# Weight loads issued by GpSimd instead of SyncE, and a later place for readers of fresh transfers, in a two-layer decoder step

## Chip, core and metric

The kernel runs on one core of a Trainium2 chip. The metric is the device time of one execution in microseconds (us), given as the median of three runs. In the views, PE is TensorE (its matmuls), PEld its weight loads, DVE VectorE, ACT ScalarE, POOL GpSimd, and SP SyncE, which here does nothing but issue DMAs. "SPq" and "POOLq" are the queues of instructions of these engines. L190 is the line of the program at which the scheduler of the kernel before calls every instruction, so nearly all rows have this line, and the tile names tell them apart.

## What is computed

One inference step of a two-layer hybrid decoder for a prompt of 512 tokens and, with the same weights, 8 further sequences of one token each (together T = 520 columns). The width is 1024.

```python
def hgrn2_chunked(q, g, k, v, S0):
    # S_t = diag(f_t) S_{t-1} + k_t v_t^T, o_t = S_t^T q_t, with g = log f, k = 1 - f
...
def hgrn2_mixer(xn, w_in, lb, onorm_g, w_out, S0):
    q, fpre, i, z = jnp.split(xn @ w_in, 4, axis=-1)
    q = jax.nn.silu(q)
    f = lb + (1.0 - lb) * jax.nn.sigmoid(fpre)
    o, S = hgrn2_chunked(heads(q), heads(jnp.log(f)), heads(1.0 - f), heads(i), S0)
    o = rmsnorm(o, onorm_g) * jax.nn.silu(z)
    return o @ w_out, S
...
def trunk(x, p, pos, hgrn_state, k_past, v_past, ...):
    for l in range(DEPTH):                      # DEPTH = 2
        xn = rmsnorm(h, pre_norm_g[l])
        if l < N_A_LAYERS:                      # layer 0: HGRN2, 16 heads of 128
            mix, S = hgrn2_mixer(xn, w_in_a[l], lb_all[l], onorm_a[l], w_out_a[l], S0)
        else:                                   # layer 1: 32 query heads of 64, 4 K/V heads, window 128
            k_sh, v_sh = jnp.split(rmsnorm(h, kv_norm_g) @ w_kv, 2, axis=-1)
            q, z = jnp.split(xn @ w_in_b[j], 2, axis=-1)
            o = window_attn_prompt(rope(q), rope(k_sh), v_sh, sinks[j])    # or window_attn_sample
            mix = (o * jax.nn.silu(z)) @ w_out_b[j]
        h = h + rmsnorm(mix, post_norm_g[l])
        h = h + (p[l] @ w_pe[l]) * jax.nn.sigmoid(h @ w_pg[l])
```

All inputs and outputs are float32.

## The kernel before

**Tiles.** Activations lie with their features on the 128 partitions and the 520 tokens along a row; a 1024-wide activation is eight such tiles. A projection makes one 128-row block of its output at a time: for each of the eight chunks of the contraction it multiplies a 128x128 block of weights with the activations, in two halves of 260 columns (`Step.mm`). To keep float32 accuracy, weights and activations are each split into a high and a low part, and three products are summed: high by high, low weight by high, high weight by low. In the rows these are `pj<-xs,wh`, `pj<-xs,wl` and again `pj<-xs,wh`, each twice for the two halves.

**Weights.** One raw weight tile `wr` is 128x1024 float32, 512 KB, and holds the eight 128x128 blocks of one output block. There are three `wr` buffers. `Step.piece` (line 600) issues its load and has `Step.halves` (line 641) split it in two pieces of 512 columns: ACT casts the piece to the high part `wh`, then DVE or POOL subtracts to get the low part `wl` (`nc.either`, which lets the scheduler choose between the two). A raw buffer is free once both of its pieces are split. Four buffers hold `wh`, four `wl`; weights of `spare` kind use tiles of another pool. `Step.stream` (line 566) walks over all output blocks and enters the pieces ahead of their use as the buffers allow. The first two pieces are special: piece 0 comes in two quarters (`begin_piece`), piece 1 in a half load.

**The first layer.** For each of 16 heads four projections (q, f, v, z) are streamed, and beside them runs the chain of an earlier head (`Step.hgrn`, line 964): scaled copies and masked products, and products `ph` on TensorE. Some operands must be transposed. `Step.turn` (line 914) does it by a round trip through memory: DVE transposes blocks into `tmp`, one DMA writes `tmp` to the DRAM tile `td`, and four DMAs read it back into `xr`. The part for the 8 sequences (`sample_a`) has further transfers of up to 512 KB (`sd`, `sb`, `in_state`). The head's norm ends in a power on POOL (`hnr`). Then follow the product with W_out, the norm over all features (`rstd`, with the power `rsr` on POOL between two products of TensorE) and the gate by `w_pe` and `w_pg`. The second layer has the same frame around windowed attention. The norm is done for the two halves of the columns apart, so `rsr` occurs twice for each norm.

**What sets the order.** Nothing is issued while the program is written. `Plan.enter` records every operation with its dependences and a price for each engine that may run it; `Plan.issue` (line 231) then simulates the whole program. It has a clock for each engine, chooses at each step the operation that can begin first (`choose`, line 259; ties go by level and by age), advances the clock by its price, and issues it. What results is one fixed list of instructions per engine, and each engine works through its list in order; an instruction that waits holds up all behind it. A DMA takes 0.45 us of its queue's clock, and its data are taken to be there 1.6 us after a modelled pipe has moved them. For TensorE `choose` already puts back operations whose operands were ready for less than HAND = 0.3 us. `self.second` is the number of the operation with which the second layer begins, `low` the oldest operation not yet issued. All DMAs are issued by SP, 777 of them; 151 are loads of `wr`.

Of the kernel before, what the change touches and what calls it, by code (L numbers as in the profile page):

```python
# [55 lines left out]
LAT = {"tensor": 0.28, "vector": 0.2, "scalar": 0.25, "gpsimd": 0.17}  # L56
HAND = 0.3

BEGIN = {"tensor": 0.9, "vector": 0.8, "scalar": 2.0, "gpsimd": 0.7, "sync": 0.0}

IDLE, SLOW = 3.4, 6.8
LATE = 1.5

RUNS = ((64, 4.0), (128, 2.0), (256, 1.4), (512, 1.15))
BACKLOG, CALM = 1.5, 40.0
# [27 lines left out]
class Plan:  # L93
# [46 lines left out]
    def price(self, engine, op, aps, a, k):  # L140


        size = max(int(np.prod(x.shape[1:])) for x in aps)
        if engine == "sync":
            run = min(self.run(x) for x in aps)
            return aps[0].nbytes() / 3.3e5 * next((f for n, f in RUNS if run <= n), 1.0), False
# [33 lines left out]
        t = 0.07 + 0.00104 * size + part  # L180
# [4 lines left out]
    def enter(self, on, name, a, k):  # L185
# [4 lines left out]
        op = Op(len(self.ops), self.level, on, [lambda c=c: c(*a, **k) for c in calls],  # L190
                [self.price(e, name, ins, a, k) for e in on], on[0] == "sync")
        if any(x.tensor.name.startswith("tw") for x in ins[1:]):
# [38 lines left out]
    def issue(self):  # L231
# [27 lines left out]
        def choose(e):  # L259
# [12 lines left out]
            able = [x for x in able if x[0] <= t]  # L272
            able.sort(key=lambda x: (e == "tensor" and x[2] + HAND > t, rank[x[1].level], x[1].n))
            if e == "gpsimd":
# [20 lines left out]
        while todo:  # L295
# [16 lines left out]
            if op.dma:  # L312
                t = max(t, lanes[0])
                clock[e] = t + 0.45
                pipe = max(pipe, t + 1.4) + cost
                op.end = pipe + 1.6 + op.late
                lanes = lanes[1:] + [op.end]
            else:
                if e == "tensor":
                    if t - clock[e] > IDLE:  # L320
                        slow = t + SLOW
                    if t < slow:
                        cost *= 2
                op.end = clock[e] = t + cost
                if held:
                    port = op.end
                    stale.update(("vector", "gpsimd"))
# [119 lines left out]
class Step:  # L447
# [152 lines left out]
    def piece(self, order, n):  # L600
# [6 lines left out]
        if w.raw is None or n < 2:  # L607
# [3 lines left out]
            sl = slice(cols[0] * PIECE, (cols[-1] + 1) * PIECE)  # L611
            self.nc.sync.dma_start(w.raw[:, sl], w.src[:, sl])
        w.pieces[half] = self.halves(w.raw[:, half * PIECE : (half + 1) * PIECE], w.spare)
# [1219 lines left out]
```

## Time and profile before

| what | value |
|---|---|
| median of 3 runs | 1070.82 us |
| lowest, highest | 1068.94, 1073.45 us |
| profiled execution, its own time | 1070.85 us |
| span of its trace | 1069.1 us |
| instructions in the span | 23985 |
| moved by the DMA queues | 178.99 MB, mean 167 GB/s |

The profiled execution's time is longer than its span by what lies before the first and after the last recorded instruction. The chain that ended last, followed back from the end of the program, is split by engine, and by the instructions with the largest shares:

```profile
PE 80%; DVE 7%; ACT 4%; DMA 4%; SPq 2%; issue 2%; POOLq 0%; POOL 0%; ACTq 0%; DVEq 0%
PE pj L190 62%; PE ph L190 18%; SPq L190 2%; DVE tmp L190 1%; DMA xr<-td 1%; DVE wl L190 1%; DVE xr L190 1%; ACT g L190 1%; ACT sb L190 1%; DVE g L190 1%; ACT wh L190 1%; DMA g<-pe 1%; DVE b L190 1%; DMA sb<-in_state 1%; ACT og L190 1%
```

A row of grouped instructions reads: line, engine, operation, what it writes <- what it reads, shape, count | busy us in all, mean ns of one | us of idle time of the engine just before them, and who ended most of it. A row of the instructions in order reads: start in us, duration, engine, line, operation, and in brackets the idle time before it and who ended it. A row of a table by windows reads: window, its length, and busy us (and count) of PE, PEld, DVE, ACT and POOL, then the granted clock of TensorE, the mean busy share of the DMA engines and GB/s. A row of a wait view reads: who waited <- for whom: us in all, times, longest us.

### The profile page before, as it was taken

To read this page: it belongs to the slowest core of one execution; us is meant where nothing else is said; L and a number is where in the kernel's file an instruction comes from. 1 tells how busy PE (TensorE), PEld (TensorE's weight loads), DVE (VectorE), ACT (ScalarE), POOL (GpSimd) and SP (SyncE) were. 2 spreads that over 40 slices of the span, in tenths; PEclk is the share of its full clock that TensorE was granted. 3 is DMA by queue.
4 is the path that set the end of the run, shared out by engine and by line. 5 is a ranking of instruction groups with operands and counts; after the bars stand their busy time and mean duration, and the time that the engine had idled before them with its cause. 6 is when DMAs were issued, how large, how long until landed. Compare 5 with 4: busy or idle time off the path is not lost.

```text
span 1069.1 us, 23985 instructions
## 1 busy us (share of the span) xinstructions
PE 1057.8 (99%) x8828; PEld 1051.2 (98%) x8828; DVE 905.4 (85%) x1971; ACT 684.1 (64%) x1829; POOL 111.7 (10%) x190
## 2 busy tenths in 40 slices
PE   9999999999999999999999999999999999999998
PEld 8999999999999999999999999999999999999998
DVE  8898788874877858778889999699999998999894
ACT  7877667665767647677736565477667654675542
POOL 1111111101111002111110000000100000002000
PEclk9999999999999999999999999999999999999999
DMA  9566656664756647676664454644433556423422
GB/s 302 185 199 199 175 167 216 191 195 142 221 155 208 195 140 217 181 209 194 198 200 160 151 190 136 176 115 138 122 103 118 156 156 190 147 89 117 162 100 81
DMA packets 147069, 178.99 MB, mean 167 GB/s; under 512 B 76932, under 2 KB 99660, under 8 KB 146952
## 3 DMA queue, kind: packets, MB, share of 16 engines
q1 hardware_dynamic: 146952, 177.46, 54.7%
q8 instruction: 70, 1.15, 0.5%
q14 instruction: 47, 0.39, 0.1%
HBM read 137.04 MB, written 34.86 MB: 161 GB/s over the span
## 4 chain that ended last, share of the span: by engine, by line
PE 80%; DVE 7%; ACT 4%; DMA 4%; SPq 2%; issue 2%; POOLq 0%; POOL 0%; ACTq 0%; DVEq 0%
PE pj L190 62%; PE ph L190 18%; SPq L190 2%; DVE tmp L190 1%; DMA xr<-td 1%; DVE wl L190 1%; DVE xr L190 1%; ACT g L190 1%; ACT sb L190 1%; DVE g L190 1%; ACT wh L190 1%; DMA g<-pe 1%; DVE b L190 1%; DMA sb<-in_state 1%; ACT og L190 1%
## 5 line engine op out<-in xcount | busy, mean ns | idle before, releaser
L190 PE MATMUL pj<-xs,wh 128*128 128x260 f32 (+2 forms) x3264 | 556.8, 285 | 1.5 <-ACT xs L190 1.3
L190 PEld LDWEIGHTS pj<-xs,wh 128*128 128x128 f32 x3264 | 458.4, 189 | 2.9 <-ACT xs L190 2.0
L190 PE MATMUL pj<-xs,wl 128*128 128x260 f32 (+2 forms) x1632 | 340.7, 285 | 0.0
L190 PEld LDWEIGHTS pj<-xs,wl 128*128 128x128 f32 x1632 | 255.2, 188 | 0.2
L190 ACT CAST wh<-wr 128x512 fp32r<-128x512 f32 x287 | 176.6, 619 | 107.7 <-PE pj L190 97.4
L190 DVE TENSOR_TENSOR wl<-wr,wh 128x512 fp32r<-128x512 f32 x273 | 186.6, 685 | 55.9 <-ACT wh L190 54.8
L190 PE MATMUL pj<-og,wh 128*128 128x260 f32 x1056 | 183.3, 285 | 0.5 <-ACT og L190 0.5
L190 PEld LDWEIGHTS pj<-og,wh 128*128 128x128 f32 x1056 | 149.7, 188 | 1.3 <-ACT og L190 0.7
L190 PE MATMUL pj<-og,wl 128*128 128x260 f32 x512 | 106.3, 284 | 0.4 <-DVE wl L190 0.4
L190 PEld LDWEIGHTS pj<-og,wl 128*128 128x128 f32 x512 | 79.9, 188 | 0.6 <-DVE wl L190 0.6
L190 ACT ACTIVATE sb<-sb,g 128x128 f32<-128x128 f32 x128 | 65.8, 560 | 6.6 <-DVE sb L190 6.6
L190 ACT ACTIVATE sb<-sb,nv 128x128 f32<-128x128 f32 x128 | 62.6, 559 | 0.3
L190 ACT COPY b<-g 128x256 f32<-128x256 f32 (+1 forms) x112 | 40.6, 377 | 20.4 <-DVE g L190 16.3
L190 ACT ACTIVATE b<-b,an 128x129 f32<-128x129 f32 x128 | 50.6, 398 | 4.6 <-DVE an L190 4.4
L190 ACT ACTIVATE tmp<-pj 128x520 f32<-128x520 f32 (+2 forms) x48 | 24.4, 526 | 41.8 <-PE pj L190 41.7
L190 PE MATMUL ph<-xs,b 128*128 128x256 f32 (+1 forms) x360 | 50.9, 283 | 0.0
L190 ACT COPY b<-ph 128x256 f32<-128x256 f32 (+1 forms) x80 | 27.9, 351 | 35.8 <-PE ph L190 35.2
L190 DVE TENSOR_TENSOR xr<-xr,b 128x256 f32<-128x256 f32 x96 | 40.8, 425 | 10.6 <-PE ph L190 8.2
L190 DVE COPY_PREDICATED xr<-lmask,ph 128x256 f32<-128x256 int32 x96 | 46.9, 489 | 3.0 <-PE ph L190 2.4
L190 PE MATMUL ph<-xr,b 128*128 128x128 f32 x320 | 48.8, 275 | 0.4 <-ACT b L190 0.4
L190 DVE TENSOR_TENSOR g<-g,b 128x256 f32<-128x256 f32 x96 | 41.1, 429 | 9.0 <-ACT b L190 5.7
L190 DVE TENSOR_TENSOR x<-x,pj 128x520 f32<-128x520 f32 (+2 forms) x64 | 39.6, 624 | 9.9 <-PE pj L190 9.2
(221 smaller groups left out, 1742.5 us busy)
## 6 DMA issues: line engine op xcount, KB each, us to landing
wr<-in_w_in_a SPq DMA_DIRECT2D x64, 512.0 KB, 4.6
sb<-sd SPq DMA_DIRECT2D x32, 512.0 KB, 5.5
wr<-in_w_in_b SPq DMA_DIRECT2D x32, 512.0 KB, 3.9
td<-tmp SPq DMA_DIRECT2D x45, 256.0 KB, 2.6
xr<-td SPq DMA_DIRECT2D x180, 64.0 KB, 3.8
sb<-in_state SPq DMA_DIRECT2D x16, 512.0 KB, 4.9
out_st_s<-sb SPq DMA_DIRECT2D x16, 512.0 KB, 3.2
wr<-in_w_out_a SPq DMA_DIRECT2D x16, 512.0 KB, 5.1
```

The source lines that it names most:

```text
L190: op = Op(len(self.ops), self.level, on, [lambda c=c: c(*a, **k) for c in calls], [self.price(e, name, ins, a, k) for e in on], on[0] == " ...
```

## The change

Two things are changed. First, `piece` issues the load of a raw weight by GpSimd's DMA queue from piece 3 on; pieces 0 to 2 stay on SP. 151 DMAs go to POOL's list, and SP keeps 626. In the scheduler, prices and the mark of a DMA now go by the operation's name instead of by the engine, and a DMA advances the clock of its queue by `ISSUE` (0.45 us on SP as before, 1.1 us on GpSimd). Second, in the first layer and after 40 us of simulated time, an operation for TensorE, VectorE or ScalarE that depends on a transfer whose planned arrival is less than SAFE = 1.5 us ago stands behind the other operations that could begin at the same moment. What each instruction computes is as before.

```diff
 SAME = {"tensor": -0.3, "vector": 0.05, "scalar": 0.1, "gpsimd": 0.02}
 LAT = {"tensor": 0.28, "vector": 0.2, "scalar": 0.25, "gpsimd": 0.17}
 HAND = 0.3
+SAFE = 1.5
+SHY = ("tensor", "vector", "scalar")
 
 BEGIN = {"tensor": 0.9, "vector": 0.8, "scalar": 2.0, "gpsimd": 0.7, "sync": 0.0}
 
 IDLE, SLOW = 3.4, 6.8
 LATE = 1.5
+ISSUE = {"sync": 0.45, "scalar": 0.35, "gpsimd": 1.1}
 
 RUNS = ((64, 4.0), (128, 2.0), (256, 1.4), (512, 1.15))
 BACKLOG, CALM = 1.5, 40.0
...
 
 
         size = max(int(np.prod(x.shape[1:])) for x in aps)
-        if engine == "sync":
+        if op == "dma_start":
             run = min(self.run(x) for x in aps)
             return aps[0].nbytes() / 3.3e5 * next((f for n, f in RUNS if run <= n), 1.0), False
         if engine == "tensor":
...
         ins = [x for x in (*a, *k.values()) if isinstance(x, bass.AP)]
         calls = [getattr(getattr(self.nc, e), name) for e in on]
         op = Op(len(self.ops), self.level, on, [lambda c=c: c(*a, **k) for c in calls],
-                [self.price(e, name, ins, a, k) for e in on], on[0] == "sync")
+                [self.price(e, name, ins, a, k) for e in on], name == "dma_start")
         if any(x.tensor.name.startswith("tw") for x in ins[1:]):
             op.late = LATE
         self.ops.append(op)
...
             t = min(x[0] for x in able)
             rank = RANK.get(e, OTHER)
             able = [x for x in able if x[0] <= t]
-            able.sort(key=lambda x: (e == "tensor" and x[2] + HAND > t, rank[x[1].level], x[1].n))
+            safe = SAFE if t > CALM and low < self.second else 0.0
+            fresh = lambda op: any(d.dma and d.end + safe > t for d in op.deps)
+            able.sort(
+                key=lambda x: (
+                    e == "tensor" and x[2] + HAND > t or e in SHY and fresh(x[1]), rank[x[1].level], x[1].n
+                )
+            )
             if e == "gpsimd":
                 for x in able:
                     op = x[1]
...
             cost, held = op.cost[n]
             if op.dma:
                 t = max(t, lanes[0])
-                clock[e] = t + 0.45
+                clock[e] = t + ISSUE[e]
                 pipe = max(pipe, t + 1.4) + cost
                 op.end = pipe + 1.6 + op.late
                 lanes = lanes[1:] + [op.end]
...
             cols = [half] if n < 2 else [h for h in range(2) if (w, h) in order]
             w.raw = self.plan.tile(self.wp, [P, KC * P], F32, self.name("wr"), "wr", 3)
             sl = slice(cols[0] * PIECE, (cols[-1] + 1) * PIECE)
-            self.nc.sync.dma_start(w.raw[:, sl], w.src[:, sl])
+            (self.nc.sync if n < 3 else self.nc.gpsimd).dma_start(w.raw[:, sl], w.src[:, sl])
         w.pieces[half] = self.halves(w.raw[:, half * PIECE : (half + 1) * PIECE], w.spare)
 
     def begin_piece(self, w, half):
```

Since the prices and the choice feed the simulation, the lists of all engines come out differently. Three places follow; buffer numbers are part of the names.

**The start, ACT.** The first rows of ACT's list before. `tmp_87` and `tmp_94` are the quarters of piece 0, `wr_95` and `wr_95` and `wr_98` are the raw tiles of pieces 1 and 2, `g_92` is the high part of the embedding's second input.

```order
L190 ACT_TABLE_LOAD
L190 CAST ones_r<-ones 128x128
L190 CAST wh_85<-tmp_87 128x256
L190 CAST g_92<-g_89 128x520
L190 CAST wh_85<-tmp_94 128x256
L190 CAST wh_96<-wr_95 128x512
L190 CAST wh_99<-wr_98 128x512
L190 ACTIVATE og_130<-x_104,vec 128x520
```

And in the change, where `wr_108` is the first load on POOL, whose list begins with it right behind the constant `mhalf`:

```order
L193 ACT_TABLE_LOAD
L193 CAST ones_r<-ones 128x128
L193 CAST wh_85<-tmp_87 128x256
L193 CAST wh_109<-wr_108 128x512
L193 CAST g_92<-g_89 128x520
L193 CAST wh_85<-tmp_94 128x256
L193 CAST wh_96<-wr_95 128x512
L193 CAST wh_99<-wr_98 128x512
L193 ACTIVATE og_130<-x_104,vec 128x520
```

The cast of the first POOL-loaded weight stands ahead of `g_92`, and all that followed moves back by one row.

**The heads' chain: SP at about 130 us and PE at about 437 us.** Before, on SP. `td_403` is written and read back to `xr_401`, the operand of the product that waits at 135 us; `wr_499` and `wr_506` are weight loads, `sd` and `sb` belong to the part for the 8 sequences.

```order
L190 DMA td_403<-tmp_402 128x512
L190 DMA xr_339<-td_341 32x16x32 x3
L190 DMA sd_452<-g_424 128x8
L190 DMA sb_454<-sd_452 128x1024
L190 DMA xr_401<-td_403 32x16x32
L190 DMA sb_455<-sd_452 128x1024
L190 DMA wr_499<-in_w_in_a 128x1024
L190 DMA wr_506<-in_w_in_a 128x1024
L190 DMA xr_401<-td_403 32x16x32 x3
```

In the change, the same place on SP:

```order
L193 DMA td_403<-tmp_402 128x512
L193 DMA sd_452<-g_432 128x8
L193 DMA xr_339<-td_341 32x16x32
L193 DMA xr_401<-td_403 32x16x32
L193 DMA sd_452<-g_424 128x8
L193 DMA xr_339<-td_341 32x16x32 x3
L193 DMA sb_454<-sd_452 128x1024
L193 DMA xr_401<-td_403 32x16x32 x3
L193 DMA sb_455<-sd_452 128x1024
```

The two weight loads have left the list, and of the read-back's four DMAs one stands two rows ahead of where it stood, the other three directly ahead of `sb_455`. On PE before, the rows around the product `ph_1137<-xr_1117,xr_1134` (the one that waits at 437 us):

```order
L190 MATMUL pj_1179<-xs_176,wh_1173 128x260 x2
L190 MATMUL pj_1179<-xs_176,wl_1174 128x260 x2
L190 MATMUL pj_1179<-xs_177,wh_1173 128x260 x2
L190 MATMUL pj_1230<-xs_162,wh_1176 128x260 x2
L190 MATMUL pj_1230<-xs_162,wl_1177 128x260
L190 MATMUL ph_1137<-xr_1117,xr_1134 128x128 x4
L190 MATMUL ph_1202<-b_1107_1201,g_1171 128x2x64 x4
L190 MATMUL pj_1230<-xs_162,wl_1177 128x260
L190 MATMUL pj_1230<-xs_163,wh_1176 128x260 x2
```

In the change:

```order
L193 MATMUL pj_1179<-xs_177,wh_1173 128x260 x2
L193 MATMUL pj_1230<-xs_162,wh_1176 128x260 x2
L193 MATMUL pj_1230<-xs_162,wl_1177 128x260 x2
L193 MATMUL pj_1230<-xs_163,wh_1176 128x260 x2
L193 MATMUL pj_1230<-xs_164,wh_1176 128x260 x2
L193 MATMUL pj_1230<-xs_164,wl_1177 128x260 x2
L193 MATMUL pj_1230<-xs_165,wh_1176 128x260 x2
L193 MATMUL ph_1137<-xr_1117,xr_1134 128x128 x4
L193 MATMUL ph_1202<-b_1107_1201,g_1171 128x2x64 x4
L193 MATMUL pj_1230<-xs_166,wh_1176 128x260 x2
```

The waiting product had three products of the projection `pj_1230` ahead of it (a row with "x2" is two); it now has twelve.

**The norm after the first layer, POOL at about 577 us.** Before. `hnr`, `nnr` are powers of the heads' norms, `rsr_1530` and `rsr_1579` the powers for the two halves of the norm over all features.

```order
L190 TENSOR_TENSOR hnr_1374<-hnm_1373,mhalf 128x4
L190 TENSOR_TENSOR nnr_1455<-nnm_1454,mhalf 128x1
L190 TENSOR_TENSOR hnr_1446<-hnm_1445,mhalf 128x4
L190 MEMSET qs_1803 128x128
L190 TENSOR_TENSOR rsr_1530<-rsm_1529,mhalf 128x2
L190 TENSOR_TENSOR rsr_1579<-rsm_1578,mhalf 128x3
L190 TENSOR_TENSOR rsr_1708<-rsm_1707,mhalf 128x2
```

In the change:

```order
L193 TENSOR_TENSOR hnr_1374<-hnm_1373,mhalf 128x4
L193 DMA wr_1499<-in_w_out_a 128x1024
L193 TENSOR_TENSOR hnr_1446<-hnm_1445,mhalf 128x4
L193 DMA wr_1566<-in_w_pe 128x1024
L193 MEMSET qs_1803 128x128
L193 DMA wr_1596<-in_w_pg 128x1024
L193 DMA wr_1560<-in_w_pe 128x512
L193 DMA wr_1610<-in_w_pg 128x1024
L193 TENSOR_TENSOR rsr_1530<-rsm_1529,mhalf 128x2
L193 DMA wr_1627<-in_w_pg 128x1024
L193 TENSOR_TENSOR rsr_1579<-rsm_1578,mhalf 128x3
L193 DMA wr_1629<-in_w_pg 128x1024
L193 DMA wr_1657<-in_w_pg 128x1024
```

Loads of weights now stand between the powers; three of them directly ahead of `rsr_1530` (and one more ahead of the memset), one between it and `rsr_1579`. In the same way two loads stand between the two powers of the last norm, and three ahead of the first of them.

## The prediction

> **What bounds the kernel now.** I read the page's part 1 first, then the same figures by stage, because an average over 1069 us hides the start and the end.
>
> ```profile
> span 1069.1 us, 23985 instructions
> PE 1057.8 (99%) x8828; PEld 1051.2 (98%) x8828; DVE 905.4 (85%) x1971; ACT 684.1 (64%) x1829; POOL 111.7 (10%) x190
> 0.00:40.00 40.00, 37.35 (x292) 35.47 (x293) 33.09 (x74) 30.33 (x61) 9.44 (x27) 1.00 0.76 248
> 40.00:620.00 580.00, 577.12 (x4848) 574.85 (x4847) 475.01 (x1031) 383.66 (x965) 76.25 (x142) 1.00 0.62 187
> 620.00:1000.00 380.00, 379.43 (x3166) 377.74 (x3165) 346.61 (x739) 239.68 (x732) 23.51 (x19) 1.00 0.47 143
> 1000.00:1069.10 69.10, 63.86 (x530) 63.14 (x528) 50.66 (x130) 30.39 (x74) 2.52 (x2) 1.00 0.26 85
> ```
>
> The reader is to see PE's column (the second number of a window): in the 580 us of the first layer's body PE lacks 580 − 577.12 = 2.88 us, in the 380 us after it 0.57, in the first 40 us 2.65, in the last 69 us 5.24. Together that is 11.3 us, 1.1% of the time, and part of it, the start and the drain at the end, belongs to no transfer. The granted clock is 1.00 in each. TensorE is the bound, and the DMA engines (0.76 to 0.26 of their time) are not, except perhaps at the start. Whatever this change frees elsewhere is worth at most the PE idle time that it removes.
>
> Next, who ends PE's idle time, in the wait view for PE and in the instructions in order of time:
>
> ```profile
> PE ph L190 <- DMA xr<-td: 0.9, 2, 0.5
> PE ph L190 <- DMA sb<-in_state: 0.8, 1, 0.8
> PE ph L190 <- POOL rsr L190: 0.4, 1, 0.4
> 135.02 1.13 PE L190 MATMUL ph<-xr,xr 128*128 128x128 f32 x8 [0.81 <-DMA sb<-in_state]
> 189.65 1.02 PE L190 MATMUL ph<-xr,xr 128*128 128x128 f32 x7 [0.49 <-DMA xr<-td]
> 437.07 1.13 PE L190 MATMUL ph<-xr,xr 128*128 128x128 f32 x8 [0.45 <-DMA xr<-td]
> ```
>
> Three products of the heads' chain (`ph<-xr,xr`) wait for a transfer: 0.81 + 0.49 + 0.45 = 1.75 us. No matmul of the trace waits for a weight's load itself. The chain view has 2% of the span on SP's queue, some 24 us; that is no gain in waiting, since that part of the chain runs beside a TensorE that is 99% busy.
>
> Last, what the loads and their queue cost. These are rows of the tile view for `wr` (who ended idle time before its readers; DMA times) and of SP's wait view:
>
> ```profile
> PE pj L190: 97.4, 80
> DMA wr<-in_w_in_a: 0.9, 2
> DMA wr<-in_w_pe: 0.7, 2
> DMA to landing us min/median/max: 3.4/4.4/9.2
> SPq L190 <- DVE wl L190: 161.0, 54, 10.4
> ```
>
> The readers of raw weights wait 97.4 us for TensorE to free their destination and 1.6 us for a load. So weights are nearly always there in time. SP, however, stands 161 us waiting for a raw buffer to be freed by the subtraction `wl`, up to 10.4 us at a time, with the heads' transfers queued behind it. That is the real disorder that the change takes away.
>
> **The change part by part.**
>
> **A, loads off SP (151 of its 777 DMAs).** SP's 161 us of waiting and 151 issues leave its queue. SP is no compute engine, so the worth is only what waits for the transfers behind: the 1.75 us above, with B. The loads may now go out as soon as a buffer is free. As they were late for 1.6 us in all, that is worth nothing on TensorE beyond A and B together.
>
> **B, readers of fresh transfers last.** The three waits above are such readers. At 437 us the new order puts twelve products of the next projection in front of the one that waits (before: three); nine more, at 0.12 us each, are 1.1 us and cover the 0.45. At 135 us SP no longer has two loads in the middle of the read-back. I take all three: **−1.75 us**. The body of the layer has 2.88 us of PE idle, so more than −2.9 cannot come from here; a reordered list may as well open new holes of the same size, so the other end is +2.9. What hides the held-back readers is the projection's matmuls; where none is ready, the rule only breaks a tie and holds nothing back.
>
> **C, the loads now stand in POOL's queue, ahead of the norms' powers (`rsr`).** No load on POOL is in the trace; call the time that one holds POOL h. The nearest rows, from each side, are SP's issue (0.33 us, next fence) and POOL's longest power (1.83 us). POOL's mid-sized instruction, the 128x4 power of the heads' norm, is nearest to the middle:
>
> ```profile
> L190 POOL TENSOR_TENSOR hnr<-hnm,mhalf 128x4 f32<-128x4 f32 x16 | 16.3, 1019 | 242.4 <-DVE hnm L190 242.3
> 26.58 3.84 SPq L190 DMA_DIRECT2D wr<-in_w_in_a  x2
> 27.38 1.54 POOL L190 TENSOR_TENSOR rsr<-rsm,mhalf 128x2 f32<-128x2 f32 x2 [22.56 <-DVE rsm L190]
> 576.10 0.33 SPq L190 DMA_DIRECT2D wr<-in_w_pg  x1
> 576.91 0.70 POOL L190 TENSOR_TENSOR rsr<-rsm,mhalf 128x2 f32<-128x2 f32 x1 [21.24 <-DVE rsm L190]
> 631.49 0.33 SPq L190 DMA_DIRECT2D wr<-in_w_kv  x1
> 631.62 0.70 POOL L190 TENSOR_TENSOR rsr<-rsm,mhalf 128x2 f32<-128x2 f32 x1 [45.20 <-DVE rsm L190]
> 1015.26 0.33 SPq L190 DMA_DIRECT2D wr<-in_w_pg  x1
> 1016.51 1.83 POOL L190 TENSOR_TENSOR rsr<-rsm,mhalf 128x3 f32<-128x3 f32 x1 [7.71 <-DVE rsm L190]
> ```
>
> I take h = 1.0. In the new order the loads of these four rows stand directly ahead of these four powers. If they go out when SP sent them, the powers wait 26.58 + 1.0 − 27.38 = 0.20, 0.19, 0.87 and 0 us (1015.26 + 1.0 is before 1016.51). At 631 us the new order has six more products of 0.12 us ahead of the transpose that reads the power, which covers 0.72 of the 0.87. Sum 0.2 + 0.2 + 0.15, of which the first two are partly behind other work: **+0.4 us**. Ends: nothing at h = 0.33; at h = 1.83 it is 1.03 + 1.02 + 1.70 + 0.58 = 4.3. The 16 powers of the heads also have loads ahead, but between a head's power and the product with W_out lie whole projections; if that cover were gone, each would cost up to h.
>
> **D, the start.** The first load moves from thirteenth on SP to POOL's first row after `mhalf`, and its cast on ACT moves ahead of `g_92`:
>
> ```profile
> 0.73 0.10 POOL L190 MEMSET mhalf<- 128x8 f32 x1 [0.29 <-POOLq L1814]
> 4.82 0.63 ACT L190 CAST g<-g 128x520 fp32r<-128x520 f32 x1 [1.42 <-DMA g<-in_pT]
> 5.96 0.74 PE L190 MATMUL pj<-g,wh 128*128 128x260 f32 x4
> wr<-in_w_in_a SPq DMA_DIRECT2D x64, 512.0 KB, 4.6
> 15.20 0.39 PE L190 MATMUL pj<-og,wl 128*128 128x260 f32 x1 [0.36 <-DVE wl L190]
> 21.03 0.39 PE L190 MATMUL pj<-og,wh 128*128 128x260 f32 x1 [0.54 <-ACT og L190]
> ```
>
> POOL is free at 0.83. With h = 1.0 in place of SP's 0.35 the load lands at 0.83 + 0.65 + 4.6 = 6.1; its cast takes 0.62, `g_92` is then done at 6.7 + 0.63 = 7.3, and TensorE wanted it in the second half of the row at 5.96, about 6.2. So TensorE starts 1.1 us late. Two waits later in the start, 0.36 (the subtraction of this very weight) and 0.54, are then shorter: by 0.6 together, I estimate. **+0.5 us**. Ends: a landing in the least 3.4 makes nothing late and frees both, −0.9; the longest landing, 9.2, makes 5.7 − 0.9 = +4.8.
>
> [...]
>
> **Sum**, against the profiled execution's own 1070.85 us (span 1069.1 and 1.75 around it; the median of the runs is 1070.82, the same): 1070.85 − 1.75 + 0.4 + 0.5 = **1070.0 us**.
>
> **Rivals.** *POOL's queue becomes the bound (slower).* If h is larger, every one of the four powers is late by 4h − 2.99 in all (0.80, 0.81, 0.13 and 1.25 us of room), and the start by h − 1 more. With B's gain the sum is 5h − 5.24, over 0.5% (5.35 us) from h = 2.1 on; at h = 3, it is +9.8, **1080.6 us**. For it: TensorE already waits for `rsr`, and at 631 us the room is 0.13. Against: POOL is busy for 10% only, and none of its rows is over 1.83.
>
> *The loads come late (slower as well).* DVE is busy for 91% of 620 to 1000 us, and if that kept POOL from preparing loads, the lead would be eaten. It decides when landing goes from 4.4 us to about three times that, since three raw buffers turn over some 7 us apart; a late load then costs its excess, and 5 us at two loads give **1080 us**. Against: only 1.6 us are lost now, and the buffers come free 7 us earlier than needed. [...]
>
> *Denser matmuls (faster).* Busy is not peak: the body has 580 us / 4848 = 119.6 ns a matmul, and its best stretch is denser:
>
> ```profile
> 480.00:520.00 40.00, 40.00 (x341) 40.00 (x340) 34.61 (x80) 28.33 (x70) 9.28 (x19) 1.00 0.63 178
> ```
>
> At 40/341 = 117.3 ns the body would take 568.7 us, 11 less. Half of that gives **1064.5 us**. Against: the difference is mostly the mix of shapes, which does not change.
>
> *The change does nothing*: loads were never late, so 1070.8; it lies inside my forecast.
>
> **How the numbers follow.** 0.5% is about what a measurement of this kernel can tell from no change. Forecast and no effect: 0.72, with 1066 to 1075 as its own range (A to D at the ends that may meet). Slower, the first two rivals: 0.18 (POOL's queue 0.12, late loads 0.06). Faster: 0.10. The range goes down to the faster rival's 1064.5 and up to 1079, which is h of 2.7, and leaves some 0.15 out.
>
> **What would show it.** In the changed trace the three `ph<-xr,xr` rows should have no idle time from a DMA; SP's wait for `wl` should be near nothing; a load on POOL should hold it for about 1 us; PE's idle time in 40 to 620 us should be 1 to 3 us. D is right if ACT's second 128x520 cast begins near 6.7 us and TensorE idles about 1 us before 8 us. I am wrong if PE's waits for `rsr`, or for `wl` and `wh`, grow by over 3 us.

## The result, and the profile after

The changed kernel takes **1093.41 us** (median of 4 runs, 1090.67 to 1095.58) against 1069.88 us of the kernel before (4 runs, 1067.22 to 1073.45). The ratio is 1.0227, with a 95% interval from 1.0208 to 1.0245: it is slower by 2.3%, some 24 us. The prediction was 1070.0 us with a range up to 1079.

The page's part 1 and part 3 of the changed kernel, in the same columns as before (part 3 is queue, kind, packets, MB, share of the time of 16 DMA engines):

```profile
span 1093.7 us, 24071 instructions
PE 1069.9 (98%) x8828; PEld 1061.4 (97%) x8828; DVE 909.4 (83%) x1973; ACT 682.7 (62%) x1829; POOL 193.3 (18%) x339
q1 hardware_dynamic: 125208, 98.55, 31.3%
q0 software_dynamic: 21680, 78.92, 21.6%
```

TensorE runs the same 8828 products. Its busy time is up by 12.1 us (1057.8 before) and its idle time by 12.5 (from 11.3 to 23.8). So half of the loss is waiting, and half is products that take longer; most of the latter, some 9.5 us, is the mean granted clock of 0.9913 over the span. The loads are now 78.92 MB on a queue of their own.

By stage, cut where the same products fall (the body of the first layer is 20 us longer):

```profile
0.00:40.00 40.00, 36.54 (x265) 34.67 (x266) 32.57 (x70) 27.50 (x54) 10.99 (x29) 1.00 0.69 240
40.00:640.00 600.00, 586.11 (x4845) 582.21 (x4844) 474.31 (x1025) 383.80 (x968) 130.50 (x234) 0.99 0.60 181
640.00:1020.00 380.00, 379.16 (x3160) 377.06 (x3159) 347.61 (x744) 239.51 (x733) 45.51 (x68) 1.00 0.47 143
1020.00:1093.70 73.70, 68.11 (x566) 67.41 (x564) 54.88 (x138) 31.87 (x78) 6.34 (x9) 0.99 0.25 87
```

The reader is to see three things. In the first 40 us 265 products begin instead of 292, which at 0.12 us each is up to 3.2 us (the same start has 276 in another execution, e1 below). The body needs 600 us for 4845 products where 580 us held 4848 before, and its granted clock is below 1. The second layer's 380 us hold 3160 products (3166 before): next to nothing was lost there.

Who ends the idle time of TensorE and of SP (wait views of PE and SP):

```profile
PE ph L193 <- DMA xr<-td: 11.0, 6, 3.1
PE ph L193 <- POOL rsr L193: 0.8, 2, 0.5
SPq L193 <- DVE wl L193: 2.3, 5, 0.6
```

And a load on POOL, by the page's groups (part 5) and issues (part 6, KB each and us from issue to landing):

```profile
L193 POOL DMA_DIRECT2D wr<-in_w_in_a x64 | 36.0, 563 | 207.7 <-DVE wl L193 171.6
wr<-in_w_in_a POOLq DMA_DIRECT2D x64, 512.0 KB, 4.5
```

SP no longer waits for raw buffers (161.0 us before, 2.3 now), just as the change meant. Yet the products `ph<-xr,xr` now wait 11.0 us for read-backs, six times and up to 3.1 us, where it was 0.9 us. A load takes no longer to land than on SP (4.5 against 4.6 us).

One such wait in the instructions in order. On POOL two loads go out at 190.09 and 192.76 us; on SP, of the two read-backs in the row at 191.66, the first is sent by 192.3 and the second takes until 197.0; TensorE then waits for it.

```profile
190.09 0.59 POOL L193 DMA_DIRECT2D wr<-in_w_in_a  x1 [0.23 <-DVE xr L193]
192.76 0.53 POOL L193 DMA_DIRECT2D wr<-in_w_in_a  x1 [2.08 <-DVE wl L193]
191.66 5.31 SPq L193 DMA_DIRECT2D xr<-td  x2
197.01 0.64 SPq L193 DMA_DIRECT2D xr<-td  x1
201.16 1.19 PE L193 MATMUL ph<-xr,xr 128*128 128x128 f32 x4 [2.37 <-DMA xr<-td]
```

The tile view gives the shortest, median and longest sending of a read-back, in ns. Before:

```profile
L190 SPq DMA_DIRECT2D xr<-td x180: 318/569/2156, 39.7 to 548.6; - x180
```

After:

```profile
L193 SPq DMA_DIRECT2D xr<-td x180: 319/569/4628, 42.7 to 571.1; - x180
```

The median has not moved; single ones in a burst now hold SP for up to 4.6 us. From sending to landing they take 1.7/3.9/9.1 us (shortest, median, longest, where the tile view can tell) against 1.7/3.8/9.0 before: what this view shows to have grown is the sending of single ones.

What such a wait costs beyond itself, around the longest one (it ends at 136.69 us):

```profile
128.00:132.00 4.00, 4.00 (x36) 4.00 (x35) 1.32 (x4) 2.25 (x5) 0.00 (x0) 1.00 0.87 228
132.00:136.00 4.00, 1.55 (x13) 1.34 (x12) 4.00 (x8) 3.76 (x9) 0.00 (x0) 0.99 1.09 237
136.00:140.00 4.00, 3.31 (x15) 3.34 (x16) 1.53 (x6) 1.53 (x5) 0.54 (x1) 0.50 0.90 303
140.00:144.00 4.00, 4.00 (x26) 4.00 (x25) 2.45 (x7) 2.05 (x7) 0.00 (x0) 0.65 0.11 36
144.00:148.00 4.00, 4.00 (x36) 4.00 (x35) 3.40 (x5) 3.07 (x12) 1.03 (x1) 1.00 0.35 132
```

The DMA engines are fully busy (1.09) while TensorE waits. A full share alone is no wait, though: in the kernel before it is 1.12 from 128 to 132 us, and 35 products begin in these 4 us. From 135.96 us on the granted clock is 0.50 for 6.83 us, and TensorE issues 15 and 26 products in 4 us where it issues 36 at full clock. Such stretches are most of the other half of the loss.

### The profile page after: what moved, and what is told of

Same layout as the page of the kernel before. It is cut to its first block, busy times and chain, and to the rows that moved or that the text cites. A ratio compares the mean times of both kernels' runs of the same rounds, so it can differ in the third digit from the quotient of the medians.

```text
span 1093.7 us, 24071 instructions
## 1 busy us (share of the span) xinstructions
PE 1069.9 (98%) x8828; PEld 1061.4 (97%) x8828; DVE 909.4 (83%) x1973; ACT 682.7 (62%) x1829; POOL 193.3 (18%) x339
## 3 DMA queue, kind: packets, MB, share of 16 engines
q0 software_dynamic: 21680, 78.92, 21.6%
## 4 chain that ended last, share of the span: by engine, by line
PE 80%; DMA 7%; DVE 4%; SPq 4%; ACT 3%; issue 2%; POOL 1%; DVEq 0%; POOLq 0%; ACTq 0%
PE pj L193 60%; PE ph L193 20%; DMA xr<-td 5%; SPq L193 4%; DMA td<-tmp 1%; ACT g L193 1%; DVE wl L193 1%; DVE x L193 1%; DVE g L193 1%; DVE tmp L193 1%; ACT tmp L193 0%; DVE acc L193 0%; ACT wh L193 0%; DVE lmask L193 0%; DMA qd<-g 0%
## 5 line engine op out<-in xcount | busy, mean ns | idle before, releaser
L193 POOL DMA_DIRECT2D wr<-in_w_in_a x64 | 36.0, 563 | 207.7 <-DVE wl L193 171.6
L193 PE MATMUL ph<-xr,xr 128*128 128x128 f32 x256 | 41.8, 289 | 11.0 <-DMA xr<-td 11.0
L193 DVE TENSOR_TENSOR xr<-xr,b 128x256 f32<-128x256 f32 x96 | 40.6, 423 | 12.1 <-PE ph L193 10.1
```

## The experiments

All ratios are against runs of the kernel before on the same chip; differences in us are the ratio less one, times 1069.5. "Waits" is TensorE's wait for `xr<-td` and `sb<-in_state` in the profiled execution; "start" is the number of products begun in the first 40 us. Both are of one execution each, which is not always near the median: e1's is its fastest (1088.59 us), e3's its slowest (1094.24).

| kernel | median us | ratio, 95% interval | waits us | start |
|---|---|---|---|---|
| before | 1068.7 to 1070.5 | 1 | 1.7 | 292 |
| the change | 1093.41 | 1.0227, 1.0208 to 1.0245 | 11.0 | 265 |
| e1 loads on GpSimd, no rule | 1093.23 | 1.0217, 1.0187 to 1.0247 | 6.6 | 276 |
| e2 rule alone, loads on SP | 1068.74 | 0.9986, 0.9973 to 1.0000 | 0 | 293 |
| e3 order of before, loads on GpSimd | 1090.70 | 1.0204, 1.0176 to 1.0232 | 14.3 | 272 |
| e4 order of the change, loads on SP | 1072.99 | 1.0034, 1.0024 to 1.0045 | 0.4 | 286 |
| e5 as e3, loads after earlier read-backs | 1092.09 | 1.0213, 1.0181 to 1.0245 | 7.8 | 272 |
| e6 GpSimd waits, loads on SP | 1070.02 | 1.0004, 0.9988 to 1.0020 | 0.4 | 298 |
| e7 GpSimd loads in the second layer only | 1073.58 | 1.0040, 1.0027 to 1.0054 | 0.9 | 278 |
| e8 the change, first loads on SP | 1091.28 | 1.0207, 1.0175 to 1.0239 | 10.9 | 278 |
| e9 one GpSimd load at the end | 1072.26 | 1.0030, 1.0018 to 1.0042 | 4.2 | 269 |
| e10 as e3, a quarter of the bytes | 1072.47 | 1.0015, 1.0005 to 1.0025 | 0.6 | 270 |
| e11 as e10, on SP | 1067.14 | 0.9971, 0.9960 to 0.9983 | 0 | 292 |
| e12 rule at 3 us, loads on SP | 1074.94 | 1.0041, 1.0029 to 1.0053 | 0 | 285 |
| e13 as e5, loads held through bursts | 1135.78 | 1.0611, 1.0584 to 1.0638 | 3.6 | 270 |
| e14 as e9, masks later | 1070.54 | 1.0018, 1.0006 to 1.0029 | 0.2 | 293 |
| e15 rule, masks later, loads on SP | 1075.38 | 1.0056, 1.0041 to 1.0072 | 0 | 293 |
| e16 as e3, SP takes its turn | 1103.26 | 1.0306, 1.0286 to 1.0326 | 8.5 | 269 |

### Which half of the change: e1 to e4

e1, the change without the rule:

```diff
-            safe = SAFE if t > CALM and low < self.second else 0.0
-            fresh = lambda op: any(d.dma and d.end + safe > t for d in op.deps)
+            fresh = lambda op: False
```

> The changed kernel without the second part (no operation stands back because its transfer is fresh); the loads stay on GpSimd. Two theories for the 24 us. Q (queue): loads that go out on a second queue as soon as a raw buffer is free now run beside the read-backs of the round trips, these land late, TensorE idles and its clock drops. O (order): the rule for fresh transfers put the operations into an order in which the round trips begin later. Q expects 1085 to 1097 us and 8 to 14 us of TensorE waiting for xr<-td. O expects 1070 to 1076 us (what is left is the start, some 3 us) and under 3 us of that wait.

e2, the kernel before with the rule:

```diff
+            safe = SAFE if t > CALM and low < self.second else 0.0
+            fresh = lambda op: any(d.dma and d.end + safe > t for d in op.deps)
...
-            able.sort(key=lambda x: (e == "tensor" and x[2] + HAND > t, rank[x[1].level], x[1].n))
+                    e == "tensor" and x[2] + HAND > t or e in SHY and fresh(x[1]), rank[x[1].level], x[1].n
```

> The kernel before with the rule for fresh transfers alone; all loads stay on SP at 0.45 us an issue. Q expects 1067 to 1073 us, TensorE's wait for xr<-td under 2 us, the granted clock at 1.00 in every stretch of 40 us. O expects 1083 us or more with 6 us or more of that wait.

e3, the kernel before; the plan still thinks of SP, only the call differs, so all lists but SP's and POOL's are as before:

```diff
-            self.nc.sync.dma_start(w.raw[:, sl], w.src[:, sl])
+            op = self.nc.sync.dma_start(w.raw[:, sl], w.src[:, sl])
+            if n >= 3:
+                op.calls = [lambda: self.tc.nc.gpsimd.dma_start(w.raw[:, sl], w.src[:, sl])]
```

> The kernel before with its planned order unchanged on TensorE, VectorE and ScalarE; only the call that issues a raw load from piece 3 on goes to GpSimd, at the same place of the program. Q expects 1083 to 1097 us with 6 us or more of TensorE's wait for xr<-td, since nothing but the queue is changed and the overlap is the same as in the changed kernel. O expects 1069 to 1075 us.

e4, the change's plan with SP as the sender:

```diff
-            (self.nc.sync if n < 3 else self.nc.gpsimd).dma_start(w.raw[:, sl], w.src[:, sl])
+            op = (self.nc.sync if n < 3 else self.nc.gpsimd).dma_start(w.raw[:, sl], w.src[:, sl])
+            op.calls = [lambda: self.tc.nc.sync.dma_start(w.raw[:, sl], w.src[:, sl])]
```

> The changed kernel's planned order (rule, prices, GpSimd's 1.1 us in the plan) on TensorE, VectorE and ScalarE, but every raw load is issued by SP, at the same place of the program. Q expects 1068 to 1076 us: SP sends loads and read-backs one after the other again; TensorE's wait for xr<-td under 4 us. O expects 1085 us or more.

All four came out as the theory of the queue has it. The queue alone costs 2.04% (21.8 us) and the order alone 0.34% (3.6 us), together 25.4 us where the change measures 24.3. Only e1's wait, 6.6 us, is a little under the 8 expected. The body of the first layer from 40 to 600 us, in e2:

```profile
40.00:600.00 560.00, 558.39 (x4697) 556.65 (x4696) 455.68 (x979) 368.75 (x932) 79.31 (x150) 1.00 0.63 191
```

In e3:

```profile
40.00:600.00 560.00, 544.65 (x4530) 542.31 (x4529) 435.56 (x930) 359.92 (x902) 121.13 (x223) 0.99 0.63 184
```

In e4:

```profile
40.00:600.00 560.00, 557.26 (x4679) 554.96 (x4679) 454.17 (x976) 368.02 (x928) 82.34 (x146) 1.00 0.63 191
```

4697 products, 4530 and 4679 (4682 before): only the kernel with loads on GpSimd falls behind, by 152 products or 18 us. In e2 the three waits of the kernel before are gone, and no product waits for a read-back.

### What it is about the queue: e5 to e7, e10, e11

e5, loads wait for the read-backs ahead of them (`polite` is called ahead of each load; `backs` holds the read-backs sent since the last):

```diff
+    def polite(self):
...
+                self.tc.keep_in_program_order(
+                    self.nc.gpsimd.tensor_tensor(self.touch[p, :1], dst[p, :1], dst[p, :1], op=ALU.mult)
+                )
```

> As e3 (planned order of before, loads on GpSimd), and GpSimd reads one column of every transposed tile whose read-back stands ahead in the program, before it sends the next load: so a load cannot move beside a read-back that was sent before it. Adds 48 or so groups of tiny GpSimd products whose result nobody uses. Three theories for the cost of the queue. V (overlap): loads move beside the read-backs of the round trips, which land late. W (GpSimd blocked): GpSimd stands waiting for a raw buffer and its own products and powers come late. G (a price per load on GpSimd, wherever it stands). V expects 1069 to 1078 us, TensorE's wait for xr<-td and sb<-in_state under 4 us together (14.3 in e3), the start still late by 2 to 3 us. W and G expect 1088 us or more, W more than e3, as GpSimd waits longer.

It stayed at 1092.09 us with 7.8 us of waiting. The theory of the overlap is not refuted by it, because the edit did not part them: in its trace the two loads of the burst at 186 us still go out at 186.9 and 189.3 us, in the middle of read-backs sent from 183.6 to 190.5, as these stand behind the loads in the program. Inconclusive.

e6, GpSimd waits for every raw buffer, and SP loads it:

```diff
+                def load():
+                    self.tc.keep_in_program_order(real.gpsimd.memset(w.raw[:, sl.start : sl.start + 1], 0.0))
+                    return real.sync.dma_start(w.raw[:, sl], w.src[:, sl])
```

> The kernel before, loads on SP, but GpSimd sets one column of each raw buffer just ahead of its load (the load overwrites it), so GpSimd stands waiting for every raw buffer as in e3, with no second DMA queue. V and G expect 1068 to 1075 us. W expects 1083 us or more, with TensorE waiting for what hangs on GpSimd's products and powers.

1070.02 us, the same as before. That GpSimd stands waiting for buffers ahead of its own work costs nothing here.

e7, only `in_w_kv`, `in_w_in_b` and `in_w_out_b` by GpSimd:

```diff
+            if w.src.tensor.name in ("in_w_kv", "in_w_in_b", "in_w_out_b"):
+                op.calls = [lambda: self.tc.nc.gpsimd.dma_start(w.raw[:, sl], w.src[:, sl])]
```

> The kernel before, with only the 52 loads of the second layer's own weights (key and value, input and output projections) issued by GpSimd, the planned order unchanged. That layer has no such read-backs of transposed heads. V expects 1068 to 1073 us. G expects 52/151 of e3's 21 us, that is 1076 to 1079 us. W expects something between, 1071 to 1077 us.

1073.58 us, just above V's range and inside W's. Its stages show why: from 640 to 1000 us 3005 products begin, against 3003 before, so 52 loads on GpSimd cost nothing there. What it lost lies at the start (278 products, 292 before), 600 us ahead of its first such load, and around the key and value tiles (318 products from 600 to 640 us, 332 before).

e10 cuts the bytes of e3's loads to a quarter, e11 does the same on SP (three quarters of each weight are left out, so both compute with other weights):

```diff
+            if w.cut:
+                sl = slice(0, PIECE // 2)
...
+        two = bass.AP(raw.tensor, raw.offset, [raw.ap[0], (0, 2), (1, PIECE // 2)])
+        nc.scalar.copy(by2(hi), two)
```

> The kernel before with the loads from piece 3 on issued by GpSimd, and each of these loads brings a quarter of its bytes (128x256 instead of 128x1024); the splits read these 256 columns four times over, so the weights are not the true ones and the output is not the reference's. Number, place and waits of the loads are as in e3 (about the same planned order), only their bytes are cut. V (loads beside read-backs take their transfer time) expects 1068 to 1077 us and TensorE's wait for transfers under 3 us. G (each DMA of GpSimd costs something by itself, whatever it moves) expects 1086 to 1094 us.

> The control to e10: the same quarter loads and the same planned order, but issued by SP. V expects 1064 to 1069 us, some 3 us (the late start) to 8 us below e10. G expects the same 1064 to 1069 us, 20 us below e10.

Body of the first layer, in e10:

```profile
40.00:600.00 560.00, 557.46 (x4689) 555.51 (x4688) 456.28 (x977) 371.95 (x933) 125.71 (x229) 1.00 0.47 135
```

In e11:

```profile
40.00:600.00 560.00, 558.20 (x4701) 556.86 (x4700) 457.12 (x986) 371.44 (x934) 76.96 (x142) 1.00 0.47 134
```

With a quarter of the bytes, the same number of GpSimd loads costs 5.3 us against its control (1072.47 and 1067.14) instead of 21.8, and about half of these is the start (270 products instead of 292, 2.6 us). In the body 12 products are left of 152. So it is the bytes that the loads move on the second queue, not their number, their issue or GpSimd's waiting.

### Time of sending, or sharing: e13 and e16

e13, a load between the write of a round trip and its last read-back is put behind that read-back:

```diff
+            if op.raw and (self.open or self.held):
+                self.held.append(op)
...
+                if op.back[1] == 3:
+                    self.open.discard(op.back[0].tensor.name)
+                    while self.held and not self.open:
+                        self.send(self.held.pop(0))
```

> As e5, and a load that stands between the write of a round trip and the last of its four read-backs is put behind that read-back in the program (unless a split needs it first), so that it is sent when the read-backs have landed. 41 of the 151 loads are held so. If loads cost time because they move beside the read-backs, then 1070 to 1078 us, TensorE's wait for xr<-td and sb<-in_state under 4 us (14.3 in e3, 7.8 in e5), with the start still 2 to 3 us late. If the second queue costs whenever it moves full loads in this layer, 1085 us or more. If the held loads come too late, TensorE waits for wh or wl instead, by over 3 us.

1135.78 us, far outside what any theory gave. The wait view of PE:

```profile
PE ph L193 <- DVE b L193: 15.4, 7, 4.4
PE ph L193 <- ACT tmp L193: 12.3, 2, 6.9
PE ph L193 <- ACT b L193: 7.7, 3, 3.8
PE ph L193 <- DMA xr<-td: 3.6, 2, 2.7
```

And of POOL:

```profile
POOL touch L247 <- DMA xr<-td: 218.4, 30, 15.4
```

The wait for read-backs fell to 3.6 us as expected, but the edit brought a new one: TensorE waits for the heads' chain on DVE and ACT. That chain hangs on GpSimd's products for each head, and GpSimd now stands 218.4 us at read-backs, up to 15.4 us at a time, with those products behind; that the one makes the other is my reading. The experiment moved the cost instead of removing it, and doesn't tell the two theories apart.

e16 keeps e3's loads and has SP wait at their old places in its list, with a 4-byte transfer behind a flag of GpSimd:

```diff
+                def load():
+                    keep(real.gpsimd.dma_start(w.raw[:, sl], w.src[:, sl]))
+                    keep(real.gpsimd.memset(flag, 0.0))
+                    return real.sync.dma_start(out, flag)
```

> As e3 (planned order of before, full loads on GpSimd's queue), and at each load's old place in SP's list SP now sends a 4-byte transfer that waits until GpSimd has sent the load. SP again stands waiting where it did in the kernel before, at the same number of issues, and sends the read-backs behind a load only after that load; only the load's bytes go by the other queue. T (the time of sending: loads sent while a burst of read-backs is under way, which SP's turn prevented) expects 1069 to 1076 us, the start's 2 to 3 us among it, and under 4 us of TensorE waiting for xr<-td and sb<-in_state. S (sharing: transfers of two queues slow each other down, whenever they are sent) expects 1083 to 1093 us and 8 us or more of that wait.

1103.26 us, more than either theory expected. Three rows of its wait views, PE's and SP's:

```profile
PE ph L190 <- DMA xr<-td: 8.5, 3, 4.1
PE ph L190 <- DMA flago<-flag: 5.0, 2, 3.3
SPq L623 <- POOL flag L622: 331.0, 106, 10.8
```

SP stands waiting again, for 331 us (161 before), and the waits for read-backs are still there. But the edit does not part the two theories: it makes SP wait for GpSimd, not GpSimd for SP. One burst in order of time, first in the kernel before, then in e16 (POOL, then SP):

```profile
151.52 5.48 SPq L190 DMA_DIRECT2D xr<-td  x6
157.05 1.88 SPq L190 DMA_DIRECT2D wr<-in_w_in_a  x2
```

```profile
152.08 0.62 POOL L621 DMA_DIRECT2D wr<-in_w_in_a  x1
155.56 0.54 POOL L621 DMA_DIRECT2D wr<-in_w_in_a  x1 [2.78 <-DVE tmp L190]
154.89 10.22 SPq L190 DMA_DIRECT2D xr<-td  x6
165.21 0.78 SPq L623 DMA_DIRECT2D flago<-flag  x2
```

Before, SP sends the two loads behind the six read-backs. In e16 GpSimd sends them at 152.08 and 155.56 us, into the burst, while SP's turns for them come from 165.2 us on; e3 sends them at 152.25 and 155.44 us. The six read-backs take 5.48 us to send before, 9.84 in e3 and 10.22 in e16. The loads ahead of the waits at 202 and 235 us were sent early in the same way. So the time of sending was not put back, and whether it is this time or the second queue as such that costs stays open. The total is no measure of either: from 640 to 1000 us e16 begins 2923 products (3003 before, 2996 in e3), so some 10 us of its loss lie in the second layer.

### The start: e8, e9, e14

e8, the change with the first 12 pieces on SP and GpSimd's DMAs planned from 30 us on:

```diff
-            (self.nc.sync if n < 3 else self.nc.gpsimd).dma_start(w.raw[:, sl], w.src[:, sl])
+            (self.nc.sync if n < 12 else self.nc.gpsimd).dma_start(w.raw[:, sl], w.src[:, sl])
...
+                    if op.dma and e == "gpsimd":
+                        held = 30.0
```

> The changed kernel with the loads of the first 12 pieces on SP and none on GpSimd before 30 us of the plan. It tells the start's share apart from the body's. All theories of the queue expect 1087 to 1092 us: 2 to 4 us less than the changed kernel's 1093.4, with 285 or more of TensorE's products begun in the first 40 us (265 in the changed kernel, 292 before). If the late start were only a consequence of a busy memory, without the early load of a weight, the count would stay under 275.

1091.28 us, but 278 products instead of 285 or more, and the change's early load is not what they lack: e1, whose start has the same lists as the change, has 276. So the start is late by 14 to 27 products from one execution to another, early load or not. The traces of e3, e5, e7 and e8 had one thing in common at the start, which e9 tests with the program's last load alone:

```diff
+            if w.src.offset == self.i["w_pg"][1, KC - 1].offset and w.src.tensor.name == "in_w_pg":
+                op.calls = [lambda: self.tc.nc.gpsimd.dma_start(w.raw[:, sl], w.src[:, sl])]
```

> The kernel before, with only the very last load of the program, 40 us before its end, issued by GpSimd. In all six kernels so far that hold a DMA of GpSimd, even where the first one comes at over 600 us, VectorE's first mask operation took 2.6 to 2.7 us (0.56 in the four without) and TensorE began late. Theory P (presence): one DMA of GpSimd anywhere in the program does this. It expects 2.6 us for that operation, 272 to 280 products begun in the first 40 us, and 1071 to 1073 us. The rival, that loads near the start do it, expects 0.56 us, 292 products and 1068.5 to 1070.5 us.

It is so. VectorE and TensorE in order of time, first the kernel before, then e9:

```profile
1.78 0.89 DVE L190 TENSOR_SCALAR lmask<-lmask 128x256 int32<-128x256 int32 x2 [0.77 <-POOL lmask L190]
5.25 0.48 PE L190 MATMUL pj<-g,wh 128*128 128x260 f32 x2 [0.69 <-DVE g L190]
```

```profile
1.79 4.12 DVE L190 TENSOR_SCALAR lmask<-lmask 128x256 int32<-128x256 int32 x6 [0.77 <-POOL lmask L190]
6.73 0.77 PE L190 MATMUL pj<-g,wh 128*128 128x260 f32 x2 [1.86 <-DVE g L190]
```

With one GpSimd DMA, at 1049 us, VectorE's first mask operation lasts 2.73 us instead of 0.56, until GpSimd has finished its run of index rows at about 4.4 us; TensorE's first real product comes 1.5 us later, and 269 products begin instead of 292 (272 to 280 forecast). The median, 1072.26 us, is where the theory had it. The three waits for transfers in the body (4.2 us together) are in that one profiled execution, whose own time, 1076.55, is the longest of its 12 runs; the start is what the median can be read for.

e14 moves the mask operations alone:

```diff
+                    if e == "vector" and any(x.startswith("lmask") for x in op.tiles):
+                        held = max(held, 12.0)
```

> As e9 (one load by GpSimd at the very end), with VectorE's 12 mask operations planned behind 12 us, so that they no longer stand ahead of the first splits while GpSimd writes its index rows. If the late start is VectorE's first mask operation held until GpSimd pauses, TensorE's gap at 4.5 us shrinks from 2.28 us to 1.2 or less, 286 or more products begin in the first 40 us (269 in e9, 292 before), and the time is 1068 to 1071 us. If a GpSimd DMA in the program slows the start in another way, the gap stays above 1.8 us and the time at 1071 to 1074 us.

293 products begin in the first 40 us and the gap at 4.5 us is gone: the late start does go through these operations. The time is 1070.54 us; the ratio's interval still begins at 1.0006, as the body, whose list the edit also changed, begins 4668 products from 40 to 600 us instead of 4682.

### Is there a faster version: e12, e15

e12 is e2 with a longer time, e15 is e2 with the edit of e14:

```diff
-SAFE = 1.5
+SAFE = 3.0
```

> The kernel before with the rule for fresh transfers at 3.0 us instead of 1.5, all loads on SP. The rule alone gave 1068.74 against 1069.47 (ratio 0.9986, interval up to 1.0000), with no product waiting for a read-back. If what it saves is these three waits, there is nothing left to save: 1067 to 1070 us, the same as at 1.5 us. If holding readers back has a price of its own (VectorE and ScalarE delayed), 1071 us or more.

> The kernel before with the rule for fresh transfers at 1.5 us and the mask operations planned behind 12 us; all loads on SP, no GpSimd DMA. A candidate for a version faster than both: the rule gave some 1 us, and if the mask operations hold VectorE ahead of the first splits even without a GpSimd DMA, up to 0.8 us of the gap at 4.4 us go too. 1066 to 1069.5 us; if the moved operations collide with the splits at 12 us, 1069 to 1072 us.

Neither. e12 gave 1074.94 and e15 1075.38 us. In e12 the loss lies from 640 to 1000 us (2944 products instead of e2's 3004), in the second layer, where the rule doesn't act; in e15 it lies from 40 to 600 us (4637 instead of 4697), though the edit ends at 12 us. In both some 60 products, 7 us, are lost; that this hangs on where the planner's choices happened to fall is my guess. e2 stays the best, 1068.74 us, but its interval ends at 1.0000, and a gain of 1.5 us is smaller than what another list moved in e12 and e15.

## Why the prediction was wrong

**What bounds it.** Right that TensorE does, and that more is not to be had than its idle time. Wrong in the next clause: "the DMA engines (0.76 to 0.26 of their time) are not, except perhaps at the start". 0.62 was the mean over 580 us. The few microseconds of a burst matter, not the mean: from 132 to 136 us the share is 1.09 while TensorE waits. Nor does the share alone tell, since it is as high in a burst of the kernel before (1.12 from 128 to 132 us, with 35 products); what is sent ahead of what has to be read with it. The reading of stages that was used for TensorE was not used for the DMA engines.

**A, loads off SP: this step failed.** It said that SP's 161 us of waiting for buffers are "the real disorder that the change takes away", and that the loads' earlier sending "is worth nothing on TensorE". The first happened (2.3 us are left) and the second did not: e3, which is this step alone, costs 21.8 us (some 2.4 of it at the start, by its 272 products). I priced the sender's time and took the transfers themselves as unchanged. In one queue the 79 MB of loads and the heads' read-backs made TensorE wait 1.75 us; from a second queue the loads are sent into the bursts of read-backs, and TensorE waits 11.0 us in the change and 14.3 in e3. e10 and e11 show that it is the loads' bytes (5.3 us with a quarter of them), e6 that it is not GpSimd's waiting (1070.02 us), e7 that such loads cost nothing from 640 to 1000 us (3005 products, 3003 before), where no such read-backs are. Whether loads sent at these moments would cost as much in one queue is open, since e16 did not part the two. How a load of one queue holds up a read-back of the other is in no view here. What the traces show is that a read-back's sending stalled until loads on the other queue were almost through: from 192.3 to 197.0 us in the changed kernel (a load landed at 197.6), and from 159.2 to 163.6 in e3 (its loads were sent at 152.25 and 155.44 us, and from 163.6 to 164.1 the DMA share is down to 0.09).

**Half of the loss was not in the sum at all**: the granted clock. The prediction took a wait at its length; of the 24.6 us in the span 12.1 are longer products, most of it at half clock around waits (17.1 us at 0.50, so some 8.5).

**B, readers of fresh transfers.** Right in its mechanism, and nearly in its size: e2 has none of the three waits, and gains 0.14% (1.5 us, none to 2.9) for the 1.75 forecast. In the change it is covered up.

**C, POOL's queue ahead of the powers.** A load holds GpSimd for 0.56 us, not 1.0, and TensorE's wait for `rsr` rose from 0.4 to 0.8 us, as much as the +0.4. That fit is luck: with h = 0.56 the working gives nothing at its four places, and the new wait (0.46 us at 607 us) is for a power that is not among them and that itself waited for VectorE, with GpSimd idle for 3.67 us ahead of it. The rival built on it (h = 3) falls; e6 shows that GpSimd's waiting is hidden (1070.02 us). In e13, with GpSimd 218.4 us at read-backs, I read that cover as at its end.

**D, the start.** The chain was right in part: the load's cast stands ahead of `g_92`, which ACT begins at 7.38 us (6.7 forecast). But the start costs 1.7 to 3.2 us (14 to 27 products), not 0.5, and most of it is there without the early load (e7, e8, e9): VectorE held while GpSimd writes its index rows (2.73 us for its first mask operation in e9, 0.56 before), which the term did not know.

**The other rivals.** No matmul waited for a load, so "the loads come late" falls; that a busy VectorE keeps GpSimd from its loads was its supposition, and with VectorE busy for 91% from 640 to 1020 us the loads of `in_w_in_b` held GpSimd for 0.53 to 0.59 us each. The products became no denser (121 ns of busy time each in the body, 119 before). "The change does nothing" falls. What held, loads of a second queue that make the read-backs late, was not among them, and its sign was not named either: the waits for `rsr`, `wl` and `wh` did not grow by 3 us, while the wait for read-backs, which was to vanish, did.

## What to carry to other kernels

Before transfers go to a second queue, look at the stretches where a transfer is awaited: at the DMA share there, not at its mean, and at which transfers are sent ahead of it. One queue can be what keeps large loads behind small urgent transfers, as at 157.05 us in the kernel before. Put the sum's waits down with what follows them, since here TensorE's waits of 1.89, 2.37 and 3.15 us came with 3.4, 3.4 and 6.8 us at half clock, and one of 1.73 with none. And measure a moved queue alone, with every other list unchanged, before a planner's new order is mixed into the result.

## What was not expected of the hardware

**The half clock around a wait came in steps of 3.4 us.** Over eight kernels of this study the time at half clock after 33 gaps of TensorE (1.3 to 7.1 us from one product's start to the next) was 0, 3.4, 6.8 or 10.2 us, with nothing between. In the changed kernel these stretches begin at 135.96, 200.81, 234.95 and 607.00 us and last 6.827 us once and 3.413 three times; the last three lie 64.85, 98.99 and 471.04 us behind the first, which is 19, 29 and 138 times 3.413. The gap's length does not decide alone: in the changed kernel gaps of 2.17 and 2.65 us were each followed by 3.4 us at half clock and one of 2.01 us by none, while in e1 one of 3.84 us was followed by none. What else decides is not shown here.

**A single GpSimd DMA changed the start of the program.** In the ten kernels with a GpSimd DMA and the masks in their old place, 265 to 278 products begin in the first 40 us; in the six without, 285 to 298. VectorE's first mask operation took 2.55 us in the changed kernel and 2.73 in e9, which has one load at the end, and lasted until GpSimd paused; in the kernel before it took 0.56. Why one DMA far behind does so is open.
